# A two-layer hybrid decoder trunk: other estimated durations behind the order of emission in the attention stages

## The chip, the core and the metric

The kernel runs on one core of one Trainium2 chip. The core has five engines with queues of their own: PE (TensorE, matrix products and transpositions), ACT (ScalarE), DVE (VectorE), POOL (GpSimd) and SP (SyncE, which here issues the DMAs). The metric is device time in microseconds (us) of one execution. The kernel before takes 3074.31 us (median of 3 runs, 3070.54 to 3074.38).

## What is computed

One inference step of a trunk with two layers, for a prompt of 1024 rows and for 8 decoding requests of 4 rows each, with shared weights. All of it is float32. The model width is 1024, the MLP width 4096.

```python
# layer 0: q, k, v, xr, g = rms_norm(x) @ w_in
z = einsum('bqhd,bkhd->bhqk', q, k) * scale + bias           # 8 heads of 64
sp = where(mask, softplus(z), 0)
rest = cumsum(sp, axis=3, reverse=True) - sp                 # stick-breaking
attn = where(mask, exp(log_sigmoid(z) - rest), 0) @ v
lru  = gelu(g) * rglru(causal_conv(xr))                      # linear recurrence
x = x + concat(attn, lru) @ w_out;   x = x + square(relu(rms_norm(x) @ w1)) @ w2
# layer 1: 16 heads of dilated attention, branches (window, dilation)
#          (128,1), (512,4), (2048,16), merged by their softmax denominators
x = x + dilated(rms_norm(x)) @ w_out; x = x + square(relu(rms_norm(x) @ w1)) @ w2
```

The decoding rows attend in layer 0 to a paged cache of K and V (8 pages of 128 positions for each request), in layer 1 to a window buffer of 1024 positions. The new K and V, the convolution's state and the recurrence's state are outputs too.

## The kernel before

A dense product of float32 operands is built from float32r parts. `xh` and `xl` are the rounded input and what is left of it, `w` stands for the high and the low half of a weight, and one product takes three matrix products (xh with the high half, xl with the high half, xh with the low half). The 1056 columns of prompt and decoding rows are cut into three times 352, so that the ordinary PE instruction is `mm<-xh,w 128x352`.

The program's stages, by the trace: the recurrent branch of layer 0 up to about 213 us; the stick-breaking attention of layer 0 (213 to 686 us); the rest of the output projection and the MLP of layer 0 (740 to 1490 us); the dilated attention of layer 1 (about 1490 to 2300 us); output projection and MLP of layer 1 to the end. In an attention stage several strands of work are woven together:

- `heads`: the attention of the prompt, by pairs of heads (4 pairs in layer 0, 8 in layer 1). A pair's scores go through `sb_scores` in layer 0 and `dl_scores` and `softmax` in layer 1; the weights (tiles `sa` and `sb` for the two heads of a pair) are transposed on PE (`tr<-ident,sa`), copied out of PSUM as a high part by ACT (`u<-tr`) and as what is left by DVE (`u<-tr,u`), and multiplied with v (`pv<-u,v`).
- `projections`: q, k and v of the next pair (`mm<-xh,w`), one unit after another; a unit is q, k or v of a pair, and has 72 products (8 blocks of the model's width, three times 352 columns, three products for each). Each unit's weights arrive as `ws` by DMA, and ACT and POOL split them into the two halves `w`. The splitting is queued by `self.after(14000, self.split_w, ...)`, that is 14000 columns of estimated PE time after the DMA's issue.
- `sb_samples` and `dl_samples`: the decoding rows against their caches. In layer 0 a page of K is transposed (`tr<-ident,u`) and split into two parts; then a page of V is split by ACT and by DVE or POOL (`u<-u`), and multiplied with the weights of the decoding rows (`tr<-u,x`, two products a page, into PSUM of the transpositions' ring).
- `early_out`: the part of the output projection whose operands are ready early (`mm<-x,w`).

These strands are Python generators. `interleave` (L934) picks at each step, among those whose next piece is estimated to be ready, the one that has done the least work for its weight. In layer 0 it runs with weights (attention 85.8 or 106.6, projections 76), and for the last pair with (attention 126, decoding rows 340, early output projection 95). What is ready is told by `Clock` (L62): it keeps, in units of a PE column (1/2.4 ns), an estimated time for each engine, for each tile's last write and last use, and for the rooms of the tile rings. `Timed` (L128) charges each ACT, DVE and POOL instruction by the table `NS` (a fixed number of ns and ns per column); `mm` (L208) charges a float32r product the larger of its columns and twice its weight's columns, `tr` twice its rows. Work that another engine must do before PE can go on is an object `Later`, and runs when PE's estimated time passes its due time and its inputs are estimated to be there.

The estimate decides the order of emission and nothing else. PE, SP and POOL execute in the order of emission (`manual_schedule`); ACT and DVE are ordered by the framework's scheduler, which starts from that order, and then execute in theirs. The MLP of layer 0 and what follows the attention of layer 1 are not ordered by the estimate.

Of the kernel before, what the change touches and what calls it, by code (L numbers as in the profile page):

```python
# [12 lines left out]
R = mybir.dt.float32r  # L13
# [3 lines left out]
PSUM = bass.MemoryType.PSUM  # L17
# [3 lines left out]
SEQ = 1024  # L21
NS = 32
NT = SEQ + NS
CW = NT // 3
# [35 lines left out]
class Clock:  # L60
# [12 lines left out]
    def __getattr__(self, n):  # L73
        return getattr(self.nc, n)
# [51 lines left out]


class Timed:  # L128
    NS = {"scalar": (100, 0.82), "vector": (70, 1.04), "gpsimd": (100, 2.2), "sync": (0, 0)}

    def __init__(self, clock, e, engine):
        self.clock, self.e, self.engine = clock, e, engine
# [1 line left out]
    def __getattr__(self, n):  # L134
        f = getattr(self.engine, n)

        def call(*args, **kw):
            r = f(*args, **kw)  # L138
            aps = [a for a in list(args) + list(kw.values()) if hasattr(a, "name") and hasattr(a, "shape")]
            outs = aps[:1] + ([kw["accum_out"]] if "accum_out" in kw else [])  # L140
            if self.e == "sync":
                o = aps[0] if aps[0].space != DRAM else aps[1]
                cost = int(np.prod(o.shape)) * 4 / 360 * 2.4
                outs = [a for a in outs if a.space != DRAM]
                ins = [a for a in aps[1:] if a.space != DRAM]
            else:
                a, b = Timed.NS[self.e]
                cost = (a + b * int(np.prod(aps[0].shape[1:]))) * 2.4
                ins = aps[1:]
            self.clock.run(self.e, cost, outs, ins)  # L150
            return r
        call.timed = True
        return call
# [18 lines left out]
class Trunk:  # L172
# [35 lines left out]
    def mm(self, out, w, x, start, stop):  # L208
        self.nc.tensor.matmul(out, w, x, start=start, stop=stop)  # L209
        n = int(np.prod(x.shape[1:]))  # L210
        m = int(np.prod(w.shape[1:]))
        self.passed(max(n, 2 * m) if x.dtype == R else max(4 * n, 4 * m), [out], [w, x])

    def tr(self, out, x, ident):
        self.nc.tensor.transpose(out, x, ident)  # L215
# [126 lines left out]
    def mm3(self, ps, terms):  # L342
        n = len(terms)
        for i, (wh, wl, xh, xl) in enumerate(terms):
            mm = self.mm
            mm(ps, wh, xh, start=i == 0, stop=False)
            mm(ps, wh, xl, start=False, stop=False)
            mm(ps, wl, xh, start=False, stop=i == n - 1)
            if i < n - 1:
                yield 0, 0  # L350
# [31 lines left out]
    def norm_finish(self, st):  # L382
# [4 lines left out]
        def sums():  # L387
            ps = self.tr_ps([128, 9])
            for t in range(9):
                n = 128 if t < 8 else NS  # L390
                self.mm(ps[:n, t:t + 1], acc[:, t * 128:t * 128 + n], self.ones[:, 0:1],
# [6 lines left out]
    def spread_rstd(self, r, rstd):  # L398

        nc = self.nc  # L400
        for c in range(3):
            pb = self.tr_ps([128, 384])
            w = 0
            for t in range(3 * c, 3 * c + 3):
                n = 128 if t < 8 else NS
                self.mm(pb[:, w:w + n], r[:n, t:t + 1].to_broadcast([n, 128]),
# [4 lines left out]
    def rsqrt(self, ps, last=True):  # L411
# [6 lines left out]
        if last:  # L418
            nc.vector.memset(m[:, k:], 1.0)
            nc.vector.tensor_scalar(m[:NS, k:], ps[:NS, k:], 1.0 / D, EPS, op0=OP.mult, op1=OP.add)  # L420
        nc.scalar.activation(t, m, AF.Sqrt)
# [1681 lines left out]
```

## Time and profile before

| what | us |
|---|---|
| median of 3 runs | 3074.31 |
| the profiled execution | 3073.03 |
| its span, first to last instruction | 3071.3 |
| PE busy | 2874.8 |
| DVE busy | 1711.0 |
| ACT busy | 1258.4 |
| POOL busy | 978.9 |

The time of an execution and the span differ by under 2 us, so that what happens inside the span is nearly all of the time. PE is busy for 94% of it; what is not PE's busy time is spread over the two attention stages and the seams between stages. The granted clock of PE has a mean of 0.966 over the span, where 1 is 2.4 GHz. The sections below show the waits of PE by releaser, and the busy time of all engines in stretches that lie in one stage each.

### The profile page before, as it was taken

Reading aid. Unit: us, or ns where it says so; the run is one execution under the profiler, and the core shown is the slowest. Engines: PE = TensorE matmul, PEld = TensorE weight load, DVE = VectorE, ACT = ScalarE, POOL = GpSimd, SP = SyncE. Lnnn points to the kernel's source line nnn. Section 1 sums busy time; section 2 is a strip of 40 time slices with the busy share of each in tenths; the row PEclk is TensorE's granted clock in tenths of the full one; section 3 lists DMA queues with packets and bytes.
Section 4 is the critical chain, followed back from the end, with each engine's and each line's share of the span. In section 5 each row is a group of like instructions: output and inputs, shape, how many; then the busy total and the mean of one; then the engine's idle time right before and its main releaser. Section 6 shows DMA issues by size and latency. Waiting matters only on the chain.

```text
span 3071.3 us, 49475 instructions
## 1 busy us (share of the span) xinstructions
PE 2874.8 (94%) x18608; PEld 2757.7 (90%) x18608; DVE 1711.0 (56%) x3657; ACT 1258.4 (41%) x2505; POOL 978.9 (32%) x613
## 2 busy tenths in 40 slices
PE   7878889979999999999999989998989999999998
PEld 7778878849999999999988888897889999999998
DVE  6868887875444444433467777766673333333335
ACT  4446666654333333333344555544452222122222
POOL 2436552443333333332412222222231122121222
PEclk9889999979999999999999999998999999999999
DMA  5111127574877777761365544555631111111111
GB/s 171 42 44 34 42 86 222 166 240 133 256 246 250 251 253 251 258 206 42 120 190 187 191 148 160 188 170 191 220 119 49 48 49 42 49 43 48 49 35 64
DMA packets 366728, 426.18 MB, mean 139 GB/s; under 512 B 23878, under 2 KB 292822, under 8 KB 366488
## 3 DMA queue, kind: packets, MB, share of 16 engines
q1 hardware_dynamic: 366488, 423.01, 42.9%
q8 instruction: 147, 2.41, 0.3%
q14 instruction: 93, 0.76, 0.1%
HBM read 296.23 MB, written 126.17 MB: 138 GB/s over the span
## 4 chain that ended last, share of the span: by engine, by line
PE 63%; DVE 6%; DMA 4%; ACT 3%; issue 1%; SPq 0%; POOL 0%; ACTq 0%; DVEq 0%; POOLq 0%
PE mm L209 54%; PE tr L209 6%; DMA ws<-in_w_in_c_dram 3%; PE tr L215 2%; PE pv L209 1%; DVE sa L138 1%; DVE sb L138 1%; ACT w L138 1%; DVE u L138 1%; DVE tl L138 1%; SPq L138 0%; DVE ats L138 0%; ACT sb L138 0%; DVE mx L138 0%; ACT o L138 0%
## 5 line engine op out<-in xcount | busy, mean ns | idle before, releaser
L209 PE MATMUL mm<-xh,w 128*128 128x352 f32 x5184 | 1380.0, 333 | 14.5 <-DVE xr L138 7.4
L209 PEld LDWEIGHTS mm<-xh,w 128*128 128x128 f32 x5184 | 939.3, 192 | 24.4 <-DVE xr L138 8.6
L138 POOL TENSOR_TENSOR w<-ws,w 128x1024 fp32r<-128x1024 f32 (+1 forms) x188 | 460.6, 2450 | 1378.9 <-ACT w L138 1295.0
L209 PE MATMUL mm<-xl,w 128*128 128x352 f32 x2592 | 848.4, 327 | 2.8 <-DVE xl L138 2.8
L209 PE MATMUL mm<-th,w 128*128 128x352 f32 (+2 forms) x3072 | 742.5, 323 | 4.4 <-DVE h L138 4.4
L209 PEld LDWEIGHTS mm<-th,w 128*128 128x128 f32 x3072 | 533.1, 188 | 7.0 <-DVE h L138 6.4
L209 PEld LDWEIGHTS mm<-xl,w 128*128 128x128 f32 x2592 | 500.9, 193 | 7.7 <-DVE xl L138 3.1
L209 PE MATMUL mm<-tl,w 128*128 128x352 f32 (+2 forms) x1536 | 493.2, 321 | 0.0
L138 ACT ACTIVATE w<-ws 128x512 fp32r<-128x512 f32 (+1 forms) x376 | 220.4, 617 | 581.2 <-issue 266.7
L138 DVE TENSOR_TENSOR h<-mm,h 128x352 f32<-128x352 f32 (+2 forms) x384 | 200.4, 524 | 416.4 <-PE mm L209 415.7
L209 PEld LDWEIGHTS mm<-tl,w 128*128 128x128 f32 x1536 | 288.7, 188 | 0.0
L138 ACT ACTIVATE t<-t 128x352 f32<-128x352 f32 x192 | 95.1, 495 | 411.2 <-DVE t L138 411.2
L138 DVE TENSOR_TENSOR tl<-t,th 128x352 fp32r<-128x352 f32 x192 | 151.4, 789 | 192.5 <-ACT th L138 192.5
L138 DVE SCALAR_TENSOR_TENSOR t<-mm,rstd 128x352 f32<-128x352 f32 x192 | 100.4, 523 | 281.0 <-PE mm L209 276.5
L138 ACT ACTIVATE u<-tr 128x512 fp32r<-128x512 f32 (+5 forms) x362 | 188.0, 528 | 164.7 <-PE tr L215 139.1
L138 DVE TENSOR_TENSOR u<-tr,u 128x512 fp32r<-128x512 f32 (+3 forms) x272 | 164.7, 614 | 74.6 <-ACT u L138 71.0
L138 POOL TENSOR_TENSOR kvs<-raw,kvs 128x512 fp32r<-128x512 f32 x80 | 103.3, 1297 | 132.0 <-ACT kvs L138 60.4
L209 PE MATMUL pv<-u,v 128*128 128x256 f32 (+1 forms) x736 | 129.2, 294 | 13.1 <-DVE u L138 12.0
L209 PE MATMUL mm<-x,w 128*128 128x352 f32 x720 | 141.4, 334 | 0.1
L209 PEld LDWEIGHTS pv<-u,v 128*128 128x128 f32 x736 | 112.7, 200 | 16.7 <-DVE u L138 13.7
L209 PEld LDWEIGHTS mm<-x,w 128*128 128x128 f32 x720 | 118.2, 192 | 4.8 <-issue 1.0
L209 PE MATMUL tr<-u,x 128*64 128x128 f32 (+1 forms) x640 | 95.3, 284 | 24.0 <-DVE u L138 16.2
(286 smaller groups left out, 3796.5 us busy)
## 6 DMA issues: line engine op xcount, KB each, us to landing
kv<-kvs SPq DMA_DIRECT2D x160, 512.0 KB
U<-kv SPq DMA_DIRECT2D x160, 512.0 KB
ws<-in_w_ff_dram SPq DMA_DIRECT2D x126, 512.0 KB
raw<-in_cache_dil_k_dram SPq DMA_DIRECT2D x320, 64.0 KB
u<-in_cache_sb_k_dram SPq DMA_DIRECT2D x64, 256.0 KB
u<-in_cache_sb_v_dram SPq DMA_DIRECT2D x64, 256.0 KB
raw<-in_cache_dil_v_dram SPq DMA_DIRECT2D x64, 256.0 KB
out_dram<-u SPq DMA_DIRECT2D x48, 256.0 KB
```

What stands on the lines that cost most here:

```text
L138: r = f(*args, **kw)
L209: self.nc.tensor.matmul(out, w, x, start=start, stop=stop)
L215: self.nc.tensor.transpose(out, x, ident)
```

## The change

The change gives the estimate other durations. The fixed part for ACT goes from 100 to 170 ns, for DVE from 70 to 150 ns, for POOL from 100 to 120 ns, and the part per column a little up for ACT and POOL. A DVE instruction of at least 256 columns is charged twice per column if it is a scan, and 1.6 times if two of its inputs lie in SBUF and have its own size. An instruction that also keeps a sum (`accum_out`) is charged 130 ns more. A float32r product is charged 1.09 times its columns. No instruction is added or removed on any engine, and none changes its shape.

```diff
--- before.py
+++ after.py
@@ -126,7 +126,7 @@
 
 
 class Timed:
-    NS = {"scalar": (100, 0.82), "vector": (70, 1.04), "gpsimd": (100, 2.2), "sync": (0, 0)}
+    NS = {"scalar": (170, 0.85), "vector": (150, 1.04), "gpsimd": (120, 2.4), "sync": (0, 0)}
 
     def __init__(self, clock, e, engine):
         self.clock, self.e, self.engine = clock, e, engine
@@ -145,8 +145,12 @@
                 ins = [a for a in aps[1:] if a.space != DRAM]
             else:
                 a, b = Timed.NS[self.e]
-                cost = (a + b * int(np.prod(aps[0].shape[1:]))) * 2.4
                 ins = aps[1:]
+                c = int(np.prod(aps[0].shape[1:]))
+                if self.e == "vector" and c >= 256:
+                    big = [i for i in ins if i.space != PSUM and int(np.prod(i.shape[1:])) == c]
+                    b *= 2 if "scan" in n else 1.6 if len(big) > 1 else 1
+                cost = (a + b * c + (130 if "accum_out" in kw else 0)) * 2.4
             self.clock.run(self.e, cost, outs, ins)
             return r
         call.timed = True
@@ -209,7 +213,7 @@
         self.nc.tensor.matmul(out, w, x, start=start, stop=stop)
         n = int(np.prod(x.shape[1:]))
         m = int(np.prod(w.shape[1:]))
-        self.passed(max(n, 2 * m) if x.dtype == R else max(4 * n, 4 * m), [out], [w, x])
+        self.passed(max(1.09 * n, 2 * m) if x.dtype == R else max(4 * n, 4 * m), [out], [w, x])
 
     def tr(self, out, x, ident):
         self.nc.tensor.transpose(out, x, ident)
```

The lines behind the inserted ones move by four: the products' line is L209 before and L213 now, the transpositions' L215 and L219. Of 18,608 PE instructions some 3,500 stand elsewhere. Three places follow.

The first is on PE, in layer 0, at the passage from the third to the last pair of heads (around 378 us in the trace of before). `tr<-ident,sa` transposes the weights of one head, `pv<-u,v` is the product that reads the transposed weights of an earlier step, `mm<-xh,w` are products of the projections for the next pair. Before:

```order
L215 MATMUL tr_3374<-ident,sa_3133 128x128
L215 MATMUL tr_3374<-ident,sa_3154 128x128 x2
L209 MATMUL mm_3294<-xh_155,w_3037 128x352
L209 MATMUL mm_3294<-xl_163,w_3037 128x352
L209 MATMUL mm_3294<-xh_155,w_3038 128x352
L209 MATMUL pv_3387<-u_3327,v_569_2663 128x256
L209 MATMUL pv_3387<-u_3328,v_569_2663 128x256
L209 MATMUL pv_3387<-u_3327,v_569_2663 128x256
L209 MATMUL pv_3387<-u_3328,v_569_2663 128x256
L215 MATMUL tr_3395<-ident,sb_3220 128x128
```

Now:

```order
L219 MATMUL tr_3370<-ident,sa_3132 128x128
L219 MATMUL tr_3370<-ident,sa_3147 128x128 x2
L213 MATMUL mm_3294<-xh_154,w_2981 128x352
L213 MATMUL mm_3294<-xl_162,w_2981 128x352
L213 MATMUL mm_3294<-xh_154,w_2982 128x352
...
L213 MATMUL mm_3394<-xl_164,w_2981 128x352
L213 MATMUL mm_3394<-xh_156,w_2982 128x352
L213 MATMUL pv_3422<-u_3326,v_570_2680 128x256
L213 MATMUL pv_3422<-u_3327,v_570_2680 128x256
L213 MATMUL pv_3422<-u_3326,v_570_2680 128x256
L213 MATMUL pv_3422<-u_3327,v_570_2680 128x256
L219 MATMUL tr_3427<-ident,sb_3221 128x128
```

Between the transposition shown and the product with v stood 3 products of the projections, and now 33 (the 28 left out are such products too). Three more stood ahead of the transposition in the order of before.

The second is on ACT, in layer 1, at a passage between pairs. `w<-ws` splits a unit's weights, `qw<-qs` are small copies of queries for the decoding rows, `u<-tr` copies transposed weights out of PSUM, `sa`, `tl` and `mx` belong to the softmax. Before:

```order
L138 ACTIVATE u_20576<-tr_20572 128x384
L138 ACTIVATE qw_17024<-qs_21226 32x2x2x4 x3
L138 ACTIVATE tl_20177,mxs_20182<-tl_20177,mxs_20182 64x672
L138 ACTIVATE qw_17024<-qs_21226 32x2x2x4 x10
L138 ACTIVATE w_20556<-ws_20554 128x512 x2
L138 ACTIVATE qw_17024<-qs_21226 32x2x2x4 x3
L138 ACTIVATE sa_20588,mx_20589<-sa_20588,mx_20589 128x384
L138 ACTIVATE u_20647<-tr_20642 128x512
L138 ACTIVATE wst_20570<-tr_20650 128x5x8x4 x2
```

Now:

```order
L138 ACTIVATE u_20584<-tr_20578 128x384
L138 ACTIVATE tl_20176,mxs_20181<-tl_20176,mxs_20181 64x672
L138 ACTIVATE w_20563<-ws_20561 128x512 x2
L138 ACTIVATE sa_20587,mx_20588<-sa_20587,mx_20588 128x384
L138 ACTIVATE qw_17024<-qs_21225 32x2x2x4 x16
L138 ACTIVATE u_20658<-tr_20652 128x512
```

The two instructions that wait for the weights' DMA stood behind 13 of the 16 small copies, and now stand ahead of all 16; the copy `u` that follows on PSUM stands behind them both times.

The third is on PE at the end of layer 0's attention stage. `tr<-u,x` are products of the decoding rows' weights with pages of the cached V, `mm<-x,w` are the products of the early output projection. Before:

```order
L209 MATMUL mm_7818<-x_4313,w_6600 128x352
L209 MATMUL mm_7818<-x_4312,w_6601 128x352
L209 MATMUL tr_7713<-u_7810,x_6011 64x512
L209 MATMUL tr_7713<-u_7811,x_6011 64x512
L209 MATMUL mm_7818<-x_4345,w_6600 128x352
L209 MATMUL mm_7818<-x_4346,w_6600 128x352
L209 MATMUL mm_7818<-x_4345,w_6601 128x352
L209 MATMUL tr_7713<-u_7823,x_6011 64x512
L209 MATMUL tr_7713<-u_7824,x_6011 64x512
L209 MATMUL tr_7713<-u_7839,x_6011 64x512
L209 MATMUL tr_7713<-u_7840,x_6011 64x512
```

Now:

```order
L213 MATMUL tr_7548<-vsh_1451,wn_6076 64x512
L213 MATMUL tr_7548<-vsl_1452,wn_6076 64x512
L213 MATMUL tr_7758<-u_7692,x_6074 64x512
L213 MATMUL tr_7758<-u_7693,x_6074 64x512
L213 MATMUL tr_7758<-u_7738,x_6074 64x512
L213 MATMUL tr_7758<-u_7739,x_6074 64x512
L213 MATMUL tr_7758<-u_7759,x_6074 64x512
L213 MATMUL tr_7758<-u_7760,x_6074 64x512
L213 MATMUL tr_7758<-u_7767,x_6074 64x512
L213 MATMUL tr_7758<-u_7768,x_6074 64x512
```

The products of the early output projection stood among the pages' products up to near the end; now the last of them (into `mm_7275`) stands over a hundred rows further up, and the pages' products follow one another.

## Rows read from the trace of the kernel before

**Rows 1.** The page: busy time of each engine; granted PE clock in 40 slices.
```profile
PE 2874.8 (94%) x18608; PEld 2757.7 (90%) x18608; DVE 1711.0 (56%) x3657; ACT 1258.4 (41%) x2505; POOL 978.9 (32%) x613
...
PEclk9889999979999999999999999998999999999999
```

**Rows 2.** Windows: length; PE, PEld, DVE, ACT, POOL busy (count); PE clock; DMA.
```profile
213.00:445.00 232.00, 205.85 (x1304) 195.39 (x1305) 182.31 (x215) 145.91 (x299) 126.39 (x103) 0.94 0.14 40
445.00:650.00 205.00, 179.27 (x1480) 161.08 (x1477) 169.42 (x250) 129.69 (x239) 76.12 (x61) 0.94 0.65 205
650.00:686.00 36.00, 23.58 (x60) 8.87 (x59) 29.07 (x40) 22.14 (x38) 21.39 (x14) 0.66 0.87 282
740.00:1490.00 750.00, 744.85 (x4637) 743.76 (x4637) 321.35 (x566) 272.02 (x502) 275.73 (x150) 0.99 0.66 215
1535.00:2090.00 555.00, 515.46 (x3747) 479.65 (x3746) 391.18 (x1376) 273.14 (x672) 129.79 (x92) 0.98 0.55 176
378.00:382.00 4.00, 4.00 (x19) 4.00 (x20) 3.97 (x6) 0.60 (x1) 3.85 (x3) 0.57 0.00 0
1823.00:1830.00 7.00, 6.83 (x24) 6.40 (x25) 6.58 (x34) 3.57 (x6) 0.00 (x0) 0.58 0.04 9
```

**Rows 3.** PE's waits, 236 to 445 us: total, times, longest.
```profile
PE pv L209 <- DVE u L138: 11.3, 4, 3.8
PE tr L209 <- DVE u L138: 5.1, 3, 2.0
PE tr L215 <- DVE sa L138: 4.3, 1, 4.3
PE tr L215 <- POOL sa L138: 2.9, 3, 1.6
PE tr L215 <- DVE u L138: 0.9, 1, 0.9
```

**Rows 4.** DVE's groups by form, 210 to 740 us: busy, mean ns | idle before.
```profile
L138 DVE TENSOR_TENSOR u<-tr,u 128x512 fp32r<-128x512 f32 x112 | 75.6, 685 | 18.7 <-ACT u L138 17.5
L138 DVE TENSOR_TENSOR u<-u,u 128x512 fp32r<-128x512 f32 x42 | 39.7, 977 | 1.7 <-ACT u L138 1.5
L138 DVE TENSOR_TENSOR_SCAN f<-f,ms 128x1024 f32<-128x1024 f32 x8 | 19.0, 2379 | 1.7 <-ACT f L138 1.7
```

**Rows 5.** Timeline around 378 us, DVE, POOL, PE: start, length [idle before].
```profile
373.45 1.98 DVE L138 CAST qb<-qb 64x512 fp32r<-64x512 f32 x1
375.35 1.75 DVE L138 TENSOR_TENSOR kb<-k,kb 64x512 fp32r<-64x512 f32 x1
377.13 0.69 DVE L138 TENSOR_TENSOR u<-tr,u 128x512 fp32r<-128x512 f32 x1
377.85 0.66 DVE L138 CAST qb<-qb 64x512 fp32r<-64x512 f32 x1
...
373.14 2.00 POOL L138 TENSOR_TENSOR sb<-sb,f 128x1023 f32<-128x1023 f32 x1 [2.29 <-DVE f L138]
...
377.88 0.76 PE L209 MATMUL pv<-u,v 128*128 128x256 f32 x3 [2.88 <-DVE u L138]
```

**Rows 6.** PE's waits, 445 to 686 us.
```profile
PE tr L209 <- DVE u L138: 16.4, 13, 3.8
PE tr L215 <- DVE u L138: 9.3, 5, 5.9
```

**Rows 7.** PE's waits, 1535 to 2090 us.
```profile
PE tr L209 <- DVE u L138: 25.0, 12, 4.4
PE tr L215 <- DVE mx L138: 9.2, 15, 1.2
```

**Rows 8.** ACT's waits, 1490 to 2300 us.
```profile
ACT w L138 <- DMA ws<-in_w_in_c_dram: 62.6, 15, 7.1
```

**Rows 9.** Timeline of a passage between pairs in layer 1: SP, ACT, PE.
```profile
1808.06 0.39 SPq L138 DMA_DIRECT2D ws<-in_w_in_c_dram  x1
...
1814.72 0.44 ACT L138 ACTIVATE qw<-qs 32x16 fp32r<-32x16 f32 x2
1818.72 1.15 ACT L138 ACTIVATE w<-ws 128x512 fp32r<-128x512 f32 x2 [3.55 <-DMA ws<-in_w_in_c_dram]
...
1823.16 0.69 PE L209 MATMUL tr<-ka,qa 128*128 128x384 f32 x1 [3.46 <-DVE u L138]
```

## The prediction, made before the changed kernel ran

> **What bounds the kernel now.** I read the page's busy times first, then windows by stage, then PE's waits in each stage, and last the timeline at single waits. PE is busy for 94% of the span [rows 1], so nearly all that can be won is in the other 196 us (3071.3 − 2874.8) and in the clock. The windows tell where they lie: in the MLP of layer 0 PE is busy for 744.85 of 750 us [rows 2], and that stage and all that follows layer 1's attention keep their order. What can move is layer 0's attention (213 to 445 us: PE idle for 26 us; 445 to 686 us: 38 us) and layer 1's (1535 to 2090 us: 40 us) [rows 2]. There PE waits for DVE above all: for the low part `u`, which DVE makes from a transposition in PSUM, before a `pv` or a `tr` product [rows 3, 6, 7]. The reader is to see that no engine but PE is full in these windows: DVE has 182 of 232 us and 391 of 555 us [rows 2]. They are waits of latency: PE comes to a product too early, with too little other work ahead of it. Such work exists, the projections of the next pair, and the estimate decides where it stands.
>
> A second loss hangs on these waits. In the four us behind the wait that ends at 377.88 us PE's granted clock is 0.57, and in seven us behind the one that ends at 1823.16 it is 0.58 [rows 2, 5, 9], that is the lower of its two levels (1.2 instead of 2.4 GHz) for most of the stretch. The mean of 0.94 over 213 to 445 us is 28 us at the lower level (232 × 0.06 / 0.5), of which half, 14 us, is lost; the 0.98 over 1535 to 2090 us is 22 us, so 11 us lost. That is an upper bound of what the clock can give back there.
>
> **What the change does.** Nothing is added or removed; the cost of the instructions is the same, and only waits change. What the estimate gets: `u<-tr,u` with 512 columns was 70 + 1.04 × 512 = 602 ns and becomes 682, where the trace has 685; `u<-u,u` goes from 602 to 150 + 1.664 × 512 = 1002, where the trace has 977; the scan of 1024 columns from 1135 to 2280, where it has 2379 [rows 4]. The product of 352 columns goes from 147 to 160 ns; the MLP's 4637 products took 744.85 us, 161 ns each [rows 2]. So the new numbers are near the mean durations, and the old ones too short. The generators whose inputs come from DVE or ACT are now held back longer, and `interleave` puts projections ahead of them. I price one projection product that is added ahead of a wait at 0.161 us, and a wait can shrink by no more than its length. Three terms follow, by stage.
>
> **Term A, layer 0 from 236 to 445 us.** PE waits here are 11.3 us in 4 times for `pv`, 5.1 us in 3 for `tr`, 4.3 and 2.9 us for `sa`, and 0.9 [rows 3], 24.5 us in all. At the first place shown in the change, the passage around 378 us, the products of the projections between the transpositions that feed `u` and the `pv` that reads it go from 9 to 36 (of them 3 and 33 behind the last transposition): 27 × 0.161 = 4.3 us of cover for a wait of 2.88 us [rows 5]. At the other three `pv` the order gives 9, 18 and 12 more, 1.4, 2.9 and 1.9 us. The longest of the four waits is 3.8 us, and by their lengths I count 1.4 + 1.5 + 2.9 + 1.9 = 7.7 of the 11.3 us. The first `sa` transposition, with its wait of 4.3 us, gets 33 products more ahead (5.3 us): all of it goes, and with it the 1.6 us of the next and the 0.9 us [rows 3], 6.8 us. Two of the three `tr` waits (5.1 us) get about 0.95 us each and the third loses 0.5, so −1.4. Against that stand a few places, near 350 and 424 us, whose cover falls from 4 to 6 us down to 2 to 3 us without a wait before; I charge +2. The sum is −13.9, taken as **−14**. Bounds: −24 if all waits but those that stay go, or the clock returns its share; 0 if what fills one place is lacking at the next, as the work is only shifted.
>
> **Term B, layer 0 from 445 to 686 us.** Here filler goes the wrong way. The last product of the early output projection stands 20 us of PE work further up than before (the third place shown), and behind it the order has 107 of the pages' products `tr<-u,x`, where it had 63. Without filler this part runs as 650 to 686 us do: 60 PE instructions, about 30 pages, in 36 us with PE busy for 23.6 at a clock of 0.66 [rows 2], or 1.2 us a page, set by the splitting of pages on ACT, DVE and POOL. Some 22 pages more (44 products at two a page) at 1.2 us are 26 us. PE's own work in them, 23.58 / 60 = 0.39 us a product at that clock and 0.26 at the full one, 11 to 17 us for 44, is due at any place; the rest is idle that is new, +9 to +15, and I take **+12** as the worst. On the other side the filler isn't lost but moved up, where PE waits 25.7 us for DVE's `u` [rows 6], much of it between 445 and 610 us, at 3.8 and 5.9 us a piece; some 8 of them could go. DVE's part of the stage is the same total, 198 of 241 us busy [rows 2], and if that sets the pace nothing changes. I take **0**, bounds −8 and +12.
>
> **Term C, layer 1 from 1535 to 2090 us.** Six passages between pairs look alike. SP issues a load of weights at 1808.06, ACT waits for it from about 1815 until 1818.72 (3.55 us), and all that stands behind on ACT is late by that, the copies `u` too, then DVE's, and PE waits 3.46 us at 1823.16 [rows 9]. ACT waits so 15 times in layer 1's attention, 62.6 us in all [rows 8]. In the changed order (the second place shown) the two splits stand ahead of the 13 small copies that they stood behind. ACT so comes to the wait earlier by 13 × 0.22 = 2.9 us (two take 0.44 [rows 9]) and does them after it. For this load nothing is won on ACT. What is won is on PE: the work between the load's issue and the first product that hangs on it is 11.6 us before and 13.8 to 14.2 us now, in the order's products priced as above, and between the transposition and the product 3.5 us become 4.8 to 5.9. Capped by the order's own differences, the six waits of 3.4 to 4.4 us lose 1.2 (three times), 1.4 or 2.4 us (twice), 9.8 in all, out of 25.0 [rows 7]. The 15 waits for `mx` (9.2 us) get up to 1.9 us more cover in half of the places and 0 in the others; −3. The sum is **−13**. Bounds: −30, nearly all 34 us, if ACT's second wait of a passage goes as well (its load is issued 44 to 58 products, 7 to 9 us, earlier); 0 if the small copies behind the split delay `u` by as much as the cover grew (16 × 0.22 = 3.5 us against 2.4).
>
> The split shows nothing moved in the rest of layer 1's attention (2090 to 2300 us) that I would price. The sum is −14 + 0 − 13 = −27 against the profiled execution of 3073.0, which stands 1.3 us under the median: **3046 us**. The clock's share is not in it beyond the rounding; it is in the bounds.
>
> **Rivals.** *The gain is larger, as the clock comes with it.* If the waits of A and C vanish, so may the stretches at the lower level behind them, and 14 + 11 us come back at most; with some 20 of them the time is near 3025. For it: each half-clock stretch seen stands behind a wait of several us. Against: the waits shrink, most don't vanish.
>
> *One factor can't fit.* A cast on DVE took 1.98 us beside a POOL instruction, and the same cast 0.66 us four us later, in a gap of POOL; `kb`, with two inputs, took 1.75 us beside POOL [rows 5]. The estimate has 682 ns for that cast whatever POOL does, so exactly at the passages, where POOL works on q and k, DVE is late by up to 2.3 us more than it knows (1.98 + 1.75 against two times 0.7). Half of A and of C is lost where cover falls short by that: −13, 3059 us. The Trainium skill ("SBUF — State Buffer", "SBUF: two separate sides") says that DVE and GpSimd share a pair of ports, which whoever starts first holds for its whole instruction while the other blocks; the rows agree as to the size of the effect, and by that rule no fixed factor would do, and the time would be this rival's.
>
> *The waits only move.* ACT's wait for the weights is set by the DMA, and DVE's pace by its own queue; what the estimate puts ahead is then lacking behind. A and C are near 0, B near 0: 3073. For it speaks that all filler was in use before too; against, that PE's waits lie at a few places with 3 to 4 us each, while between them it has none.
>
> *Slower.* The pages of V at layer 0's end run bare: B at +12, while A and C give nothing because the moved filler leaves new holes: 3085. The mechanism is the pages' splitting at 1.2 us a page, which nothing covers. It decides from the point where the early projections end before the pages' last third. For it: the order shows just that. Against: A and C would have to fail at the same time.
>
> **How the numbers follow.** The forecast (its own range 3030 to 3060) has 0.48, the larger gain 0.10, the half gain 0.12, no change 0.13, slower 0.17. A measurement can tell 0.2%, about 6 us, from no change; the first three cases lie beyond it, so faster is 0.70, same 0.13, slower 0.17. The range of 8 in 10 goes from 3020 (A and C near their bounds) to 3083.
>
> **What would show it.** If A is right, PE's four `pv` waits between 236 and 445 us fall from 11.3 to under 5 us, and the window's clock rises above 0.94. If C is right, PE's waits for `u` in layer 1 fall from 25.0 to about 15 us, and ACT's for the weights stay or fall. If B is right, the stretch between 445 us and the MLP keeps its length; if it grows by 10 us with PE at a low clock and waits on `tr<-u,x`, the slower rival has come. A kernel with the same sum of PE waits, at other places, would prove the forecast wrong.

## The result and the profile after

The changed kernel takes 3036.45 us (median of 4 runs, 3035.2 to 3038.4), against 3072.43 us for the kernel before in the same comparison (3067.77 to 3074.38): a ratio of 0.9886 with a 95% interval of 0.9869 to 0.9903. The forecast was 3046, 27 us less; it became 36 us less. The range and the sign held. The sum was nearly right while two of its three terms were not, so the stages have to be read one by one.

Two lines of the changed kernel's page, busy time and granted clock, answer to [rows 1]:

```profile
PE 2855.5 (94%) x18608; PEld 2741.9 (90%) x18608; DVE 1715.8 (57%) x3657; ACT 1255.9 (41%) x2505; POOL 986.6 (33%) x613
...
PEclk9989999979999999999999999998999999999999
```

PE's busy time falls by 19 us with the same instructions, at a mean granted clock of 0.970 instead of 0.966; the other 18 of the 37.3 us of span (3071.3 − 3034.0) are idle time of PE.

For the stages, windows of both kernels are cut where PE does the same work. The cuts are the transposition `tr<-ident,oc` behind PE's wait for POOL, late in the recurrent branch, the end of the first long wait at the cached pages of K, a late product with a page of V, the MLP's start, layer 1's start, a late passage of its attention, the start of its output's split, the end. The kernel before (columns as in [rows 2]):

```profile
213.40:454.40 241.00, 207.73 (x1318) 196.88 (x1318) 191.14 (x224) 151.47 (x309) 132.84 (x109) 0.93 0.17 50
454.40:649.60 195.20, 177.00 (x1462) 159.40 (x1462) 159.79 (x242) 124.13 (x228) 69.33 (x53) 0.95 0.63 200
1490.30:2092.40 602.10, 559.42 (x4001) 522.85 (x4002) 410.29 (x1421) 291.48 (x715) 145.91 (x104) 0.97 0.54 174
```

The changed kernel:

```profile
214.20:442.50 228.30, 203.17 (x1318) 191.07 (x1319) 188.12 (x228) 149.27 (x309) 135.00 (x110) 0.97 0.19 53
442.50:649.50 207.00, 179.21 (x1463) 156.76 (x1463) 161.84 (x237) 125.47 (x232) 71.14 (x53) 0.93 0.61 195
1491.20:2054.00 562.80, 545.87 (x4000) 516.86 (x3998) 416.76 (x1420) 291.70 (x714) 147.58 (x104) 0.98 0.58 186
```

The reader is to see three differences: 241.0 to 228.3 us, −12.7, in layer 0 up to the pages (term A); 195.2 to 207.0, +11.8, at the pages (term B), which gives nearly all of A back; and 602.1 to 562.8, −39.3, in layer 1 (term C). In C PE's idle time (length less busy) goes from 42.7 to 16.9 us, and its busy time falls by 13.5 us at a clock of 0.98 instead of 0.97. The other stages move by 1 to 5 us either way. Among them the rest of layer 1's attention (2092 to 2298 us before) is 3.6 us shorter; its order changed too, which the prediction had left out.

PE's waits from 236 to 436 us of the changed kernel answer to [rows 3]:

```profile
PE tr L213 <- DVE u L138: 5.0, 4, 2.3
PE tr L219 <- ACT sa L138: 4.5, 2, 4.1
PE pv L213 <- DVE u L138: 3.7, 5, 2.4
PE tr L219 <- POOL sa L138: 1.7, 3, 1.1
```

The four `pv` waits of 11.3 us have become 3.7, and the wait of 4.3 us for DVE's `sa` is gone. A new one of 4.1 us for ACT's `sa` has come, and the `tr` waits of 5.1 us have stayed. The clock of layer 0 up to the pages rises from 0.93 to 0.97.

PE's and ACT's waits in layer 1 answer to [rows 7, 8]; first PE from 1535 to 2052 us, then ACT from 1490 to 2300 us:

```profile
PE tr L219 <- DVE mx L138: 6.6, 2, 3.5
PE tr L213 <- DVE u L138: 2.6, 6, 0.6
```

```profile
ACT w L138 <- DMA ws<-in_w_in_c_dram: 35.9, 8, 8.0
```

PE's waits for `u` were 25.0 us and are 2.6. ACT's wait for the weights' DMA fell from 62.6 us in 15 times to 35.9 in 8. What is left on PE comes in two pieces of 3 us, and one of them is this, on the queues of SP, ACT and PE (it answers to [rows 9]):

```profile
1784.27 0.61 SPq L138 DMA_DIRECT2D tt<-tv  x1
1784.93 0.59 SPq L138 DMA_DIRECT2D tf<-tv  x1
1785.62 0.51 SPq L138 DMA_DIRECT2D out_dram<-u  x1
1786.23 0.84 SPq L138 DMA_DIRECT2D U<-kv  x2
1787.16 0.39 SPq L138 DMA_DIRECT2D ws<-in_w_in_c_dram  x1
...
1798.64 1.15 ACT L138 ACTIVATE w<-ws 128x512 fp32r<-128x512 f32 x2 [7.16 <-DMA ws<-in_w_in_c_dram]
...
1802.82 0.79 PE L219 MATMUL tr<-ident,tl 64*128 64x64 f32 x6 [3.08 <-DVE mx L138]
```

The load is issued at 1787.16, ACT stands at the split until 1798.64, 11.5 us after the issue, and PE's wait of 3.08 us ends four us after that. The next load of the same pair has no wait at all:

```profile
1806.94 0.49 SPq L138 DMA_DIRECT2D mix<-o  x1
1807.53 0.54 SPq L138 DMA_DIRECT2D ws<-in_w_in_c_dram  x1
...
1812.87 1.14 ACT L138 ACTIVATE w<-ws 128x512 fp32r<-128x512 f32 x2
```

This load landed within 5.3 us, and PE runs through. So a load can take 5 or 11 us; the first is issued right behind two transfers `U<-kv`, the other behind one of `mix<-o`.

Place by place the picture is mixed. Before, ACT waited at 15 splits, and PE's longer waits for `u` (3.9, 1.4, 3.7, 0.9, 3.5, 3.5 and 4.4 us) followed seven of them; five others, of 5.3 to 7.1 us, were followed by 0.8 us of it or none. In the changed kernel ACT's wait is gone or down to 1.1 us at three of the seven places, and PE's 8.0 us there go with it. At two ACT still waits 3.7 and 3.9 us, and PE's 5.2 us are all but gone, presumably by cover. At the last two, one of them that of [rows 9], ACT's wait has grown from 3.6 and 4.5 to 7.2 and 7.6 us, and PE waits 3.1 and 3.5 us, now for `mx`.

### The profile page after: what moved, and what is told of

It reads as the page before. It is cut to its first block, busy times and chain, and to the rows that moved or that the text cites. A ratio compares the mean times of both kernels' runs of the same rounds, so it can differ in the third digit from the quotient of the medians.

```text
span 3034.0 us, 49488 instructions
## 1 busy us (share of the span) xinstructions
PE 2855.5 (94%) x18608; PEld 2741.9 (90%) x18608; DVE 1715.8 (57%) x3657; ACT 1255.9 (41%) x2505; POOL 986.6 (33%) x613
## 4 chain that ended last, share of the span: by engine, by line
PE 65%; DVE 5%; ACT 3%; DMA 3%; issue 2%; POOL 1%; SPq 0%; ACTq 0%; DVEq 0%; POOLq 0%
PE mm L213 56%; PE tr L213 6%; PE tr L219 2%; PE pv L213 1%; DMA ws<-in_w_in_c_dram 1%; DVE sa L138 1%; ACT w L138 1%; DVE u L138 1%; DVE tl L138 1%; DVE sb L138 1%; DVE xl L138 0%; DMA U<-kv 0%; ACT xh L138 0%; DVE h L138 0%; SPq L138 0%
## 5 line engine op out<-in xcount | busy, mean ns | idle before, releaser
L213 PE MATMUL mm<-xh,w 128*128 128x352 f32 x5184 | 1339.6, 330 | 20.5 <-DVE xr L138 7.3
L213 PEld LDWEIGHTS mm<-xh,w 128*128 128x128 f32 x5184 | 928.7, 191 | 30.3 <-DVE xr L138 8.4
L213 PE MATMUL mm<-xl,w 128*128 128x352 f32 x2592 | 846.4, 327 | 1.0 <-DVE xl L138 1.0
L213 PE MATMUL mm<-th,w 128*128 128x352 f32 (+2 forms) x3072 | 742.1, 323 | 6.3 <-DVE h L138 6.3
L213 PEld LDWEIGHTS mm<-th,w 128*128 128x128 f32 x3072 | 533.0, 188 | 9.2 <-DVE h L138 8.6
L213 PEld LDWEIGHTS mm<-xl,w 128*128 128x128 f32 x2592 | 496.8, 192 | 5.0 <-DVE xl L138 1.3
L213 PE MATMUL mm<-tl,w 128*128 128x352 f32 (+2 forms) x1536 | 493.5, 321 | 0.0
L213 PEld LDWEIGHTS mm<-tl,w 128*128 128x128 f32 x1536 | 288.9, 188 | 0.0
L213 PE MATMUL pv<-u,v 128*128 128x256 f32 (+1 forms) x736 | 134.6, 300 | 8.8 <-DVE u L138 8.8
L213 PE MATMUL mm<-x,w 128*128 128x352 f32 x720 | 136.9, 331 | 3.7 <-DVE k L138 2.7
L213 PE MATMUL tr<-u,x 128*64 128x128 f32 (+1 forms) x640 | 98.3, 291 | 27.3 <-DVE u L138 23.0
L213 PEld LDWEIGHTS mm<-x,w 128*128 128x128 f32 x720 | 116.8, 191 | 7.1 <-DVE k L138 3.0
L213 PEld LDWEIGHTS pv<-u,v 128*128 128x128 f32 x736 | 107.9, 197 | 13.4 <-DVE u L138 11.5
```

## The experiments

Three stretches are read from each trace, in us: layer 0 from the first transposition `tr<-ident,oc` (at 176.5 us before) to the first one of a page of K (447.0 us), from there the pages of layer 0 to the last product with a page of V, and layer 1 from the sums of its first norm to those of its second. A time is a median, a stretch comes from the one profiled execution: the seven kernels with the order of before at the pages (two of them but for four instructions) have 241.2 to 244.9 there.

| kernel | time | ratio to before, 95% | layer 0 to pages | pages | layer 1 |
|---|---|---|---|---|---|
| before (in three comparisons) | 3073.2 to 3073.5 | | 270.5 | 243.0 | 808.8 |
| after | 3036.45 | 0.9869 to 0.9903 | 256.8 | 254.5 | 768.2 |
| e1, layer 1 only | 3037.19 | 0.987 to 0.9903 | 270.8 | 243.5 | 773.6 |
| e2, old in the last weave | 3024.56 | 0.9825 to 0.9859 | 257.7 | 244.9 | 775.7 |
| e3, before, late split | 3075.64 | 0.9998 to 1.0023 | 269.9 | 242.9 | 807.5 |
| e4, after, late split | 3031.91 | 0.9854 to 0.9887 | 257.7 | 252.4 | 767.0 |
| e5, before, loads earlier | 3037.94 | 0.9873 to 0.9906 | 271.8 | 241.7 | 773.2 |
| e6, e2 with loads earlier | 3019.21 | 0.9806 to 0.9849 | 257.9 | 241.8 | 767.2 |
| e7, product's price only | 3086.3 | 1.0023 to 1.0062 | 268.9 | 247.5 | 819.1 |
| e8, kept sums only | 3085.52 | 1.003 to 1.006 | 270.2 | 241.2 | 821.4 |
| e9, fixed parts only | 3039.55 | 0.9874 to 0.9907 | 267.5 | 254.2 | 760.4 |
| e10, scans and inputs only | 3076.05 | 1.0004 to 1.0024 | 267.9 | 243.8 | 809.4 |
| e11, e6 without sums and product | 3012.61 | 0.9784 to 0.9817 | 252.7 | 246.7 | 763.0 |

**Where the gain lies: e1 and e2.** In both, and in e6 to e11, a set `ON` tells which of the new durations hold (`ns` the table of fixed parts and prices per column, `scan` and `two` DVE's factors, `acc` the kept sums, `mm` the product). e1 begins with none and takes all at layer 1:

```diff
     def layer1(self, st, rstd):
         nc = self.nc
+        Timed.ON = set(['acc', 'mm', 'ns', 'scan', 'two'])
```

> The new durations hold only from the start of layer 1's attention; layer 0 keeps the old ones, so its stage is emitted as before. If the gain is layer 1's own (the changed kernel's stretch there is 38.7 us shorter, and layer 0's is about as long as before), the time is that of the changed kernel within 5 us: 3033 to 3042, with layer 0's attention (213 to 650 us) at the length of before. If layer 0 carries half of the gain, as the prediction had it, it is near 3054.

It took 3037.19 us, the changed kernel's time, with layer 0's stretches as before (270.8 and 243.5). Layer 1 alone is worth the whole gain.

e2 takes all from the start, none in the last weave of layer 0, and all again at layer 1:

```diff
+                    Timed.ON = set([])
                     self.interleave((att, 126), (sample, 340), (early, 95))
```

> The new durations everywhere but in the last weave of layer 0 (last pair of heads, cached pages, early output projection), which gets the old ones and so its order of before, with early products among the pages of V to near the end. If that weave's 11.8 us loss comes from the new durations used there, it goes: 3021 to 3028 us, with the 12.7 us that the part before it won kept. If the filler was only shifted (what the first part wins the second must lose), the loss stays: 3034 to 3040.

3024.56 us: 11.9 us less than the changed kernel, with intervals that don't touch. The first part keeps what it won (257.7) and the pages are back at 244.9. So the loss there is not the price of what the first part won; the new durations in that weave cost the time. The pages of V do run bare, as the traces show for 610 to 650 us; the kernel before:

```profile
610.00:650.00 40.00, 34.65 (x182) 26.54 (x182) 32.64 (x55) 19.79 (x37) 14.66 (x10) 0.91 0.62 202
```

The changed kernel:

```profile
610.00:650.00 40.00, 29.90 (x108) 15.58 (x108) 31.60 (x49) 20.86 (x39) 17.68 (x12) 0.71 0.63 189
```

DVE, ACT and POOL have nearly the same busy time, but PE runs 108 instructions instead of 182, at 0.71 instead of 0.91: the early products that stood here have been used up. But this is not where the time is lost. Cut at the first product with a page of K, the first with a page of V and the last, the kernel before has

```profile
457.56:575.28 117.72, 110.95 (x1110) 106.56 (x1109) 91.48 (x135) 80.66 (x146) 31.15 (x20) 0.97 0.70 221
575.28:689.97 114.69, 91.17 (x416) 62.07 (x415) 96.48 (x140) 64.41 (x120) 57.33 (x40) 0.84 0.62 198
```

and the changed one

```profile
444.84:576.27 131.43, 118.80 (x1172) 115.09 (x1171) 95.86 (x142) 78.81 (x143) 35.16 (x24) 0.99 0.64 210
576.27:688.08 111.81, 84.85 (x354) 51.43 (x353) 98.32 (x133) 65.94 (x123) 55.12 (x40) 0.79 0.61 188
```

Some 60 early products moved from the pages of V to those of K. The pages of V got 2.9 us shorter without them, less than a third of the products' own 60 × 0.161 = 9.7 us, since PE had idle time there. The pages of K got 13.7 us longer: PE was busy there for 110.95 of 117.72 us, so that the products cost their full time, and its idle time rose from 6.8 to 12.6 us besides. e2 has 117.4 and 116.5 us in these two stretches, as before; e4, with the changed order, has 129.8 and 111.3.

**What layer 1 waited for: e3 to e6.** The first attempt at ACT's wait queues the split later, in the kernel before (e3) and in the changed one (e4):

```diff
-            return w, self.after(14000, self.split_w, *w, need=w[:1], made=w[1:])
+            return w, self.after(24000 if width == 1024 else 14000, self.split_w, *w, need=w[:1], made=w[1:])
```

> The kernel before with one number changed: in layer 1 the splitting of a unit's weights is queued 24000 instead of 14000 columns of estimated PE time after the load's issue, all durations old. If PE's waits for u in layer 1 are ACT's waits for the weights' DMA handed on, ACT's 62.6 us for it fall under 20 us, PE's 25 us for u under 10, and the time falls by 15 to 30 us, to 3043 to 3058. If the cover by other products decides, as the prediction priced it, PE's waits stay and the time is within 6 us of before or longer, since the units get ready later.

> The changed kernel with the same later splitting in layer 1. If ACT's wait for the weights is what is left there (35.9 us in 8 times, with PE waits of 3 to 3.5 us behind two of them), it goes and the time falls by 5 to 12 us, to 3025 to 3032. If cover decides, nothing: 3034 to 3040, or slower where units come late.

e3 took 3075.64 us, no difference. That decides nothing, since the treatment didn't take: in layer 1 the order on ACT, by the names of its tiles, differs from that of before in one place, where a split stands one row further down, and ACT's waits are what they were:

```profile
ACT w L138 <- DMA ws<-in_w_in_c_dram: 60.8, 15, 7.6
```

ACT is not one of the engines that stand in the order of emission, but POOL is, and its half of the splits stands where it did too; why the later due time moved so little is not shown. e4 took 3031.91 us, 4.5 less than the changed kernel and in the range of its first case, but the intervals overlap, layer 1 has 767.0 instead of 768.2, and its order on PE, SP and POOL is that of the changed kernel. ACT still waits 34.0 us in 8 times. So e4 decides nothing either.

e5 takes the wait away from the other end. In the kernel before, with all durations old, the DMA of a unit's weights is issued one unit earlier (the ring of three `ws` buffers has room for it):

```diff
+        raws = {}
+        def fetch(u):
+            raws[u] = self.raw_w(win[:, :, units[u][2]:units[u][2] + 128], 8, 128)
         def load(u):
-            w = self.load_w(win[:, :, units[u][2]:units[u][2] + 128], 8, 128)
+            if u not in raws:
+                fetch(u)
+            w = (raws.pop(u), *self.parts_w(8, 128))
...
             if u + 1 < len(units):
                 nxt = load(u + 1)
+            if width == 1024 and u + 2 < len(units):
+                fetch(u + 2)
```

> The kernel before with old durations, but in layer 1 the DMA of a unit's weights is issued one unit (72 products) earlier, so that it has landed when ACT comes to the split. If PE's waits for u in layer 1 are ACT's wait for that DMA handed on, ACT's 62.6 us fall under 15 us, PE's 25 us for u under 10, and the time falls by 15 to 35 us, to 3038 to 3058. If PE's cover decides, ACT's wait goes but PE's waits for u stay above 18 us and the time is within 6 us of before. A loss would mean that the earlier loads get in the way of the attention's own transfers.

3037.94 us, and layer 1 at 773.2: the earlier loads alone give what all the new durations give. ACT has no wait for the DMA of these weights left; what it still waits for at the splits are products of PE (4.7 us in one time before):

```profile
ACT w L138 <- PE mm L209: 24.7, 13, 4.7
```

PE's waits from 1535 to 2058 us are now:

```profile
PE tr L215 <- DVE tl L138: 4.2, 6, 0.8
PE tr L215 <- DVE mx L138: 3.6, 10, 1.0
PE tr L209 <- DVE mxs L138: 3.1, 4, 0.8
PE tr L215 <- ACT v L138: 2.2, 5, 0.7
PE tr L209 <- DVE u L138: 2.0, 6, 0.7
```

The 25.0 us for `u` are 2.0, though the cover is what it was: PE runs layer 1 in the order of before, but for one passage at 1572 to 1581 us, which e3 has too. So PE's wait for DVE's `u` was ACT's wait for a DMA, two engines further up, and a longer cover was not needed to be rid of it.

e6 adds the same earlier loads to e2.

> The kernel of e2 (old durations in layer 0's last weave, new ones elsewhere) with the same earlier loads in layer 1. If ACT's remaining 35 us of waits for the weights cost PE what follows two of them (3 to 3.5 us, at two passages, and their clock), the time falls by 5 to 12 us, to 3012 to 3020. If what is left is DVE's softmax (mx), nothing: 3021 to 3028.

3019.21 us, with layer 1 at 767.2 instead of 775.7. The step is of the expected size, but the intervals of e2 and e6 overlap, so the stage shows it and the whole time doesn't prove it. In layer 1 the new durations of e2 win 33.1 us, the earlier loads of e5 35.6, and both together 41.6: for the most part they take away the same waits.

**Which of the durations: e7 to e11.** Each of e7 to e10 has a part of them alone, through all stages: e7 `{'mm'}`, e8 `{'acc'}`, e9 `{'ns'}`, e10 `{'scan', 'two'}`.

> Only the float32r product's price is changed (1.09 times its columns), all other durations old. It makes the estimate of PE slower against the other engines, so that inputs look ready earlier in terms of products and less cover is put ahead of them: 3074 to 3090 if the rest of the change is what wins. If the product's price is the term that counts in layer 1 (the splits come due after fewer products), the time falls by over 10 us.

3086.3 us, slower as the first case had it. ACT's wait for the weights grows:

```profile
ACT w L140 <- DMA ws<-in_w_in_c_dram: 102.6, 18, 8.5
```

(In e7 to e10 the lines are shifted by two more.) A price that is nearer to the measured 161 ns makes it worse. That the other engines, still priced too low, look earlier yet beside a slower PE is the reading of the expectation; no run shows it apart.

> Only the 130 ns for instructions that keep a sum are added, all else old. They occur in layer 1's softmax alone in the attention stages, so layer 0 keeps its order there. If the gain in layer 1 is carried by the softmax's durations, 10 us or more go, to under 3063; if by the durations of u (fixed parts of ACT and DVE), nothing: within 6 us of before.

3085.52 us, which neither case had: layer 1 is 12.6 us longer. ACT's wait for its weights is 54.1 us here, less than before, so what the kept sums cost comes from elsewhere; PE now waits 12.6 us for `u` at `pv` products. Its cause stays open.

> Only the table of fixed parts and prices per column is new (ACT 170, DVE 150, POOL 120 ns fixed); scans, two inputs, kept sums and products as before. In layer 1, the product's price alone and the kept sums alone each cost 10 us or more. If the gain there is carried by the fixed parts (u's chain is ACT plus DVE, 150 ns longer), layer 1 from its first sums to its MLP falls from 808.8 us to under 785, ACT's wait for the weights' DMA from 62.6 to under 45 us, and the time is 3040 to 3060. If no part carries it and only the five together do, layer 1 stays above 800 and the time is above 3066.

3039.55 us, with layer 1 at 760.4, the best of all variants. ACT waits 32.3 us in 12 times, and PE's `u` waits are 2 us:

```profile
ACT w L140 <- DMA ws<-in_w_in_c_dram: 32.3, 12, 5.3
```

The fixed parts carry layer 1's gain, and not by ACT's waits alone: ACT still waits at 12 places, for 2.7 us on average, and PE hardly waits behind them, which leaves the cover. They also bring the loss at the pages (254.2).

> Only the factors for scans (2) and for two inputs in SBUF (1.6) are new. Scans occur in layer 0 alone. If layer 0's part before the cached pages (270.5 us before, 256.8 after) is won by them, it falls to under 262 and layer 1 moves little: 3058 to 3068. If the fixed parts win it, it stays above 267: 3070 to 3080.

3076.05 us. Layer 0's part is 267.9, so scans alone don't win it. But e9 alone has 267.5 there, so the fixed parts don't win it alone either, as the second case had it; all five together have 256.8. The parts don't add up.

e11 is e6 with `{'ns', 'scan', 'two'}` in place of all five.

> The kernel of e6 without the two parts that cost time alone: kept sums and the product's price stay old, so that new are the fixed parts, the scans and the two inputs, outside layer 0's last weave. If the parts add up, some 10 us more go: 3004 to 3013 us. If the order is a throw of the dice within some per cent once the weights no longer make ACT wait, it is within 8 us of e6 on either side: 3011 to 3027.

3012.61 us, the fastest kernel here: 2% below before, 24 us below the changed one. Its interval ends at 0.9817 where that of e6 begins at 0.9806, so that it is faster than e6 is likely and not shown. 3012.61 lies in the ranges of both cases and doesn't tell between them. Its layer 0 gains (252.7) and its pages lose a little (246.7).

## Why the prediction was right in its sum, and where it failed

**Bound by waits of latency on PE, and a clock that follows them: right.** The number of PE's instructions is the same, DVE, ACT and POOL are as busy as before, and the gain is 18 us of PE's idle time and 19 us of its busy time at a better clock.

**Term A, −14: right in size, −12.7, but made of something else.** The `pv` waits fell from 11.3 to 3.7 us, as forecast (under 5), and the clock rose above 0.94. The `sa` waits, from which I took 6.8 us, came back in part at ACT's `sa` (4.5 us), and the `tr` waits lost nothing instead of 1.4. PE's idle time (length less busy) fell by 8.1 us, from 33.3 to 25.1; the other 4.6 are busy time at a better clock, which the sum had left to the bounds.

**Term B, 0: wrong, +11.8, at its upper bound, and not by that bound's mechanism.** The prediction set up to +12 for bare pages of V, and against it a credit of 8 us, that the filler moved up would cover the waits for `u` there. The step that failed is this credit. It rests on a misreading: of the 25.7 us only 10.1 lie before 610 us, as the kernel before shows from 445 to 610 us, and 5.9 of them are one wait ahead of all early products:

```profile
PE tr L215 <- DVE u L138: 9.3, 5, 5.9
PE tr L209 <- DVE u L138: 0.8, 3, 0.4
```

Behind that wait PE had 6.8 us of idle time at the pages of K, and with the products moved there this stretch grew by 13.7 us instead of losing up to 8. The bare pages of V, at 1.2 us each, were to cost the 12; they got 2.9 us shorter. That the sum of both falls on the bound is chance. e2 shows that the loss hangs on the durations used in this weave.

The long wait at the first pages stayed, and grew from 5.9 to 7.1 us; it ends where the window of B begins and so counts in A:

```profile
442.46 1.09 PE L219 MATMUL tr<-ident,u 128*128 128x128 f32 x4 [7.08 <-DVE u L138]
```

DVE had just then two `kb` of 2.48 and 1.75 us and a row of small copies ahead of the four `u`; the early products, the filler of this weave, begin only at 457.26 us in this trace.

**Term C, −13 with a bound of −30: the direction right, the size wrong by a factor of three.** The step that failed is the cap by the order's own differences, by which the six waits lose 9.8 us in all. "For this load nothing is won on ACT" held for the load that it was read from; what failed is that the six passages look alike. I had seen ACT's wait for the weights in front of PE's wait [rows 8, 9], and then capped the gain by the added cover, as if each passage kept that wait. In the changed kernel seven of the 15 waits are gone, and PE's waits for `u` lost 22.4 us instead of 9.8. e5 shows that the wait for the DMA alone is worth 35 us, with no duration changed. (The six waits of 3.4 to 4.4 us are five in the trace; the sixth is the 1.4 us at 1653 us.) The other step is the clock: the bound of −30 was only PE's waits, 34 us less a little; 13.5 us less of busy time came on top, which the text had priced at up to 11 and left out of the sum.

**The rivals.** The larger gain through the clock came true in C. "The waits only move" did not come true: A's gain did not go to B, as e2 keeps the one without the other's loss. "Slower" gave B's number, not its mechanism.

That one factor can't fit DVE's casts beside POOL is shown, its price is not: A's gain was not halved. In the changed kernel DVE and POOL run

```profile
433.84 0.42 DVE L138 CAST qb<-qb 64x512 fp32r<-64x512 f32 x1
434.18 2.48 DVE L138 TENSOR_TENSOR kb<-k,kb 64x512 fp32r<-64x512 f32 x1
437.21 0.86 DVE L138 CAST qb<-qb 64x512 fp32r<-64x512 f32 x1
437.99 1.75 DVE L138 TENSOR_TENSOR kb<-k,kb 64x512 fp32r<-64x512 f32 x1
...
433.95 2.16 POOL L138 TENSOR_TENSOR sb<-sb,f 128x1023 f32<-128x1023 f32 x1 [3.29 <-DVE f L138]
436.08 1.71 POOL L138 TENSOR_TENSOR ql<-q,qa 64x512 fp32r<-64x512 f32 x1
437.86 1.33 POOL L138 TENSOR_TENSOR ql<-q,qb 64x512 fp32r<-64x512 f32 x1
```

The second cast ends at 438.07, 0.28 us after the POOL instruction that ran when it began (436.08 + 1.71); the two `kb` end 0.55 us after theirs. In layer 0 of both traces all 11 such casts end 0.28 or 0.29 us after POOL's instruction and all 14 such `kb` 0.55 us, however long they took; with POOL idle at their start a cast takes 0.42 us and a `kb` 0.69. So the cast of 0.66 us in [rows 5] did not run in a gap of POOL, as the prediction read it, but met the end of a POOL instruction. The Trainium skill's rule on the shared ports ("SBUF — State Buffer", "SBUF: two separate sides"), for a DVE operation in a two-port mode or with two inputs in SBUF, agrees with these rows.

That the sum came out within 10 us is luck: B's loss of 11.8 us hid nearly a third of C's 39.3.

## What to carry to other kernels

Follow a wait back past the engine that the profile names: PE waited for DVE, DVE for ACT, and ACT for a DMA that another order issues early enough or not. A wait at the head of an in-order queue is worth what stands behind it on all the engines further down, not what the last of them shows as cover; and it can be worth little, as five of ACT's longer waits here. Filler is cheap only where the engine that runs it has room: 60 products cost little at the pages of V, and more than their own time at the pages of K, where PE was nearly full. Where an estimate orders the work, a better price in one place is not a better order: two of the four parts, taken alone, made it 0.4% slower, and one part alone gave nearly all. Try such a change stage by stage, since here one stage lost what another won.

## What was not expected of the hardware

A load of 512 KB of weights landed within 5.3 us when ACT came to it at 1812.87, and after 11.5 us at 1798.64 in the same trace, with two `U<-kv` transfers issued just ahead of it. These two alone do not make the difference. In the trace of before the 15 loads that ACT waited for took 5.1 to 12.0 us from issue to split, and all but the shortest had two `U<-kv` in the 3 us ahead of them; the four of 10.7 us and more, and only they, had `tt<-tv` and `tf<-tv` there as well, as had the load of 11.5 us above. What sets the time is inferred from the order on SP's queue, not tested.
